# Turning the values and the heads' outputs by crossbar transfers and GpSimd copies in place of TensorE transposes

## The chip, the cores and the metric

The kernel runs on one core of a Trainium2 chip. Its engines work side by side: TensorE (PE, with its weight loads as PEld) multiplies, VectorE (DVE) and ScalarE (ACT) do elementwise work, GpSimd (POOL) does simple copies, and SyncE (SP) only issues DMAs. The time is that of one execution in device microseconds; the median of a few runs is given.

## What is computed

One layer of a hybrid backbone over 2048 latent tokens of width 1024, with a prefix of 256 context tokens. The part that the change touches is a bidirectional gated linear recurrence in eight heads of width 128. Cut to what matters:

```python
h = rmsnorm(x, norm_w) * (1 + scale) + shift          # (2048, 1024)
p = h @ w_in                                           # 9216 columns, f32
q, v, zf, zb = heads 0..7 of width 128, gate = the next 1024 columns
f = lb + (1 - lb) * sigmoid(z); k = 1 - f              # forward and backward
# chunkwise, per head and direction:
S_t = diag(f_t) S_{t-1} + k_t v_t^T;  o_t = S_t^T q_t
o = o_forward + o_backward                             # context first, from state 0
y_hg = o * rsqrt(mean(o*o) + eps) * onorm_w * silu(gate)
y_cv = gated short convolution of the other 4096 columns
x = x + gate_ada * (concat(y_hg, y_cv) @ w_out);  out = rmsnorm(x, final_norm_w)
```

## The kernel before

Every large product is written as three f16 products of a high and a low half, and pairs of 128-column blocks go through a seven-product scheme (`seven`, line 921), so that one unit is 7 products of 4 steps of 3 matmuls. The work is a list of windows (lines 1225 to 1311): 32 windows for eight heads times four segments of 512 tokens, then 4 windows for the first convolution block and 14 for the others, then the output projection. A window's units project the segment's gates, values and queries. Its `chain` is the scan of the segment before it, and its `extra` holds the second direction of the previous head, the scaling of its outputs and other side work. Heads alternate in the order of their segments, so that a window's operand tiles ("hops", nine buffers) are loaded as the last unit of the window before gives its buffers back (`prefetch`, line 1384).

The order is written out by a planner: every step has a weight (`PACE`, line 45), `merge_steps` (line 1437) spreads chain and extra over the window in proportion to their weights, and `tick` (line 1458) issues a step after the matmuls at its place. Each engine then works through its own instructions in that order. SyncE issues all DMAs concerned, also in that order, and an issue that has to wait for a buffer or a datum holds back those behind it.

The steps of one segment's scan (`scan_steps`, line 715) are these. `value_turn` (line 552): four TensorE transposes of 128x128 f32 (line 555) into PSUM and a ScalarE copy to SBUF (line 557), since the projection gives values with channels on partitions and the scan needs tokens there. `begin_levels`, then levels 0 to 6: each even level (`levels`, line 620) multiplies 32-wide blocks on TensorE (line 631), and every level updates the keys (`level_k`, line 485) and the queries (`level_q`, line 492) on VectorE in place. The odd levels 1, 3 and 5 (`held`, line 603) keep a copy of the keys by ScalarE (`km`, line 601) and one of the queries by GpSimd (`qm`, line 608) ahead of the update, for the matmuls of the next step. `level6` (line 641) collects the blocks with four small GpSimd copies (line 665). `key_turn`, `states` and `outp` turn the keys, form the states (line 681, which reads the values) and the outputs (line 737).

When a head's both directions are done, `y_steps` (line 813) scales a segment's output by its norm on ScalarE (line 825), turns it with four TensorE transposes (line 831), and VectorE multiplies the turned output in PSUM by the norm weight and the gate (line 833); `put_y` (line 751) takes its largest entry and stores it to DRAM.

Tiles come from rings: `ring` has ten buffers of 512 f32 per partition, and `pair` in the pool `hp` has four buffers, used by stores of the operand tiles (line 317) early on and by scans of the output weights (line 1016) in the windows of heads 6 and 7.

Of the kernel before, what the change touches and what calls it, by code (L numbers as in the profile page):

```python
# [10 lines left out]
F16 = mybir.dt.float16  # L11
BF16 = mybir.dt.bfloat16
I32 = mybir.dt.int32
U8 = mybir.dt.uint8
AF = mybir.ActivationFunctionType
ALU = mybir.AluOpType
# [3 lines left out]
P = 128  # L20
# [5 lines left out]
GW = 512  # L26
NG = SEQ // GW
NCH = GW // P
HK = KT // 2
HW = GW // 2  # L30
HOPS = 9
VQ_AT = 3
SMALL = {"cc": 16, "bada": 16, "nw": 8, "lg": 32, "onw": 1, "cw": 24}
HEADS = 8
HG = HEADS * P
# [15 lines left out]
def paced(weight, fn):  # L51

    return PACE.get(weight, weight), fn
# [7 lines left out]
def hybrid_layer(ctx: ExitStack, tc, x, cx, w_ada, b_ada, w_in, w_out, fnorm_w, small_d, masks, ident_d, sel_d, out):  # L61
    nc = tc.nc
    V, S, G, PE, SY = nc.vector, nc.scalar, nc.gpsimd, nc.tensor, nc.sync
# [8 lines left out]
    hp = hpg.__enter__()  # L72
# [24 lines left out]
    def px_t(nm):  # L97
        return px.tile([P, 512], F32, tag="px", name=nm)

    def ring(nm):  # L100
        return rp.tile([P, GW], F32, tag="ring", name=nm)
# [6 lines left out]

    def k_tile(nm):
        return scp.tile([P, 2, GW], F32, tag="K", name=nm)  # L110

    def flat(t):
        return t.rearrange("p a b -> p (a b)")
# [13 lines left out]
    def rsqrt(ss, n, inv_n, nm):  # L127
# [3 lines left out]
        V.tensor_scalar(v, ss, inv_n, EPS, ALU.mult, ALU.add)  # L131
        V.tensor_scalar(a.bitcast(I32), v.bitcast(I32), 1, None, ALU.logical_shift_right)
        V.tensor_scalar(y.bitcast(I32), a.bitcast(I32), -1.0, float(0x5F3759DF), ALU.mult, ALU.add)
        for _ in range(3):
# [5 lines left out]
    def pow2_scale(rs, nm, keep=False, room=0, rb=None):  # L140
# [7 lines left out]
        else:  # L148
            st = sp.tile([P, 4], F32, tag="scale", name=f"sc_{nm}", bufs=12)
        sti = st.bitcast(I32)  # L150
        V.tensor_scalar(sti[:, 2:3], ps[:, :1].bitcast(I32), 24, None, ALU.logical_shift_right)
        V.tensor_scalar(sti[:, 0:1], sti[:, 2:3], -EXP_UNIT, (204.0 - room) * EXP_UNIT, ALU.mult, ALU.add)
# [7 lines left out]

    small = cp.tile([P, sum(SMALL.values())], F32, name="small")
    SY.dma_start(small, small_d)
    par, at = {}, 0
    for nm_, n_ in SMALL.items():
        par[nm_] = small[:, at:at + n_]
# [4 lines left out]
    bada, nw, onw = par["bada"], par["nw"], par["onw"]  # L170
# [15 lines left out]
    def modulate(between, vq):  # L186
        pada = pa_t("pada")
        homes = [f_tile, k_tile, f_tile, k_tile, q_tile, q_tile] + [wa_hop] * 4

        def load(k):  # L190
            wa[k] = []
            for j in range(2):
                t = homes[(2 * k + j) % len(homes)](f"wa{k}{j}")
                t = t if len(t.shape) == 3 else t.rearrange("p (a b) -> p a b", a=2)
                SY.dma_start(flat(t), w_ada[0, k * P:(k + 1) * P, j * D:(j + 1) * D])
                wa[k].append(t)

        wa = {}
        room = len(homes) // 2
        for k in range(room):  # L200
            load(k)
            if k == VQ_AT:
                vq()
        for k in range(KT):
            for j in range(4):
                PE.matmul(pada[32 * j:32 * j + 32, :], sc32[:, k, :], wa[k][j // 2][:, j % 2],
                          start=k == 0, stop=k == KT - 1)
            if k + room < KT:
                load(k + room)
            between(k)  # L210
        return pada
# [261 lines left out]
    lb1 = cp.tile([P, 2, HEADS], F32, name="lb1")  # L473
    mask = qp.tile([P, NSUB, SB], U8, name="mask", bufs=1)

# [25 lines left out]
    def new_state(nm):  # L501
        return qp.tile([P, P], F32, tag="state", name=nm, bufs=10)
# [4 lines left out]
    class Seg:  # L507


        def __init__(s, hd, tok0, n, m, nm):  # L510
            s.hd, s.tok0, s.n, s.m, s.nm = hd, tok0, n, m, nm
            s.small = n < GW
            s.f = s.K = None

        def open_gates(s):
# [175 lines left out]
    def order(i, n):  # L691
        return list(range(n)) if i == 0 else list(range(n - 1, -1, -1))
# [22 lines left out]
    def scan_steps(h, s):  # L715
        prim = h.prim

        def states():
            pp = s.outer(prim)
            s.Ss = []  # L720
            Sp = h.S[prim]
            for ch in order(prim, NCH):
                s.Ss.append(Sp)
                Sn = new_state(f"S_{s.nm}_{ch}")
                V.scalar_tensor_tensor(Sn, Sp, s.decay(prim, ch), pp[:, ch * P:(ch + 1) * P], ALU.mult, ALU.add)
                Sp = Sn
            h.S[prim] = Sp
            psec = s.outer(1 - prim)
            s.Ts = scp.tile([P, GW], F32, tag="Tsec", name=f"Ts_{s.nm}", bufs=5)
            S.activation(s.Ts, psec, AF.Copy)  # L730

        def outp():
            po = px_t(f"o_{s.nm}")
            qo = (1 - prim) * GW
            for ch, Sp in zip(order(prim, NCH), s.Ss):
                sl = slice(ch * P, (ch + 1) * P)
                PE.matmul(po[:, sl], s.A[:, sl], s.v[:, sl], start=True, stop=False)
                PE.matmul(po[:, sl], s.qf[:, qo + ch * P: qo + (ch + 1) * P], Sp, start=False, stop=True)
            s.o = s.qf[:, qo:qo + GW]
            S.activation(s.o, po, AF.Copy)  # L740

        return ([paced("values", s.value_turn), paced("begin", s.begin_levels)]
                + [paced("levels", lambda: s.levels(0)), paced("held", lambda: s.held(1)),
                   paced("levels", lambda: s.levels(2)), paced("held", lambda: s.held(3)),
                   paced("levels", lambda: s.levels(4))]
                + [paced("held", lambda: s.held(5)), paced("level6", s.level6), paced("keys", s.key_turn), paced("states", states),
                   paced("out", outp)])

    ymax = cp.tile([P, 3 * HEADS, NG], F32, name="ymax")
# [1 line left out]
    def put_y(kt, g, y):  # L751
        V.tensor_reduce(ymax[:, kt, g:g + 1], y, mybir.AxisListType.X, ALU.max, apply_absolute_value=True)
        SY.dma_start(yT[g][:, kt, :], y)
# [59 lines left out]
    def y_steps(h, j, own_gate=False):  # L813
        s = h.segs[-1 - j]

        def gate():
            s.sg = qp.tile([P, GW], F32, tag="sg", name=f"sg_{s.nm}", bufs=2)
            SY.dma_start(s.sg, Gd[h.hd][:, s.tok0:s.tok0 + GW])

        def scale():  # L820
            if not own_gate:
                gate()
            for ch in range(NCH):
                sl = slice(ch * P, (ch + 1) * P)
                S.activation(s.o[:, sl], s.o[:, sl], AF.Copy, scale=h.rstd[:, j * NCH + ch:j * NCH + ch + 1])

        def turn():
            pt = px_t(f"oT_{s.nm}")
            for ch in range(NCH):
                sl = slice(ch * P, (ch + 1) * P)  # L830
                PE.transpose(pt[:, sl], s.o[:, sl], ident)
            y = ring(f"y_{s.nm}")
            V.scalar_tensor_tensor(y, pt, onw, s.sg, ALU.mult, ALU.mult)
            put_y(h.hd, s.tok0 // GW, y)

        return ([paced(0.0, gate)] if own_gate else []) + [paced("scale", scale), paced("turn_y", turn)]


    class Conv:
# [358 lines left out]
    for hd in range(HEADS):  # L1198
        h = Head()
        h.hd, h.prim, h.segs = hd, hd % 2, []  # L1200
        heads.append(h)
        h.ctx = Seg(hd, SEQ, CTX, 1, f"c{hd}")
        for i, g in enumerate(order(h.prim, NG)):
            s = Seg(hd, g * GW, GW, 0, f"{hd}_{g}")
            h.segs.append(s)

    def wkey(c0, c1, own=False):
# [19 lines left out]
    for wi, (kind, a, i) in enumerate(stretch):  # L1227
        units, chain, extra = [], [], []
        if kind == "head":
            h = heads[a]  # L1230
# [34 lines left out]
        if wi > 0 and stretch[wi - 1][0] == "head":  # L1265
            _, pa_h, pi = stretch[wi - 1]
            chain += scan_steps(heads[pa_h], heads[pa_h].segs[pi])
# [377 lines left out]
def _arrays(inputs):  # L1645
# [7 lines left out]
         "in_w_in": i_["w_in"][0].reshape(KT, P, -1, P).transpose(2, 1, 0, 3), "in_w_out": i_["w_out"],  # L1653
         "in_final_norm_w": i_["final_norm_w"], "in_small": np.concatenate([cols[n] for n in SMALL]).T}
    a.update(_constants())
# [3 lines left out]
def _constants():  # L1659
    p = np.arange(P)  # L1660
    diff = (p[:, None] % SB) ^ np.arange(SB)[None, :]
    m = np.zeros((P, NSUB, SB), np.float32)
    for lev in range(NSUB):
        m[:, lev, :] = (diff >> lev) == 1
    sel = np.zeros((P, 2, P), np.float32)
    for j in range(2):
        sel[[32 * j, 64 + 32 * j, 32 * j + 2], j, :] = 1.0
    return {"level_masks": m.reshape(P, NSUB * SB), "identity": np.eye(P, dtype=np.float32),
            "selector": sel.reshape(P, 2 * P)}
# [15 lines left out]
```

## Time and profile before

| | |
|---|---|
| Median of 3 runs | 2149.38 us (2148.78 to 2149.49) |
| The profiled execution (its span) | 2150.1 us |
| TensorE busy | 2073.2 us, 96% |
| VectorE busy | 1645.8 us, 77% |
| ScalarE busy | 1192.2 us, 55% |
| GpSimd busy | 191.8 us, 9% |
| Granted TensorE clock, mean | 0.994 |

Busy time is the union of an engine's instructions. A matmul's duration overlaps that of its neighbours in the pipeline, so the place that it takes in PE's order is read from the start of one to the start of the next. "Idle before, releaser" names what ended the idle time of an engine: for line 631 it may be GpSimd's copy of held queries or VectorE's update. The windows of the eight heads end near 1265 us; the turns that the change concerns begin with the eighth segment, near 374 us for the values.

### The profile page before, as it was taken

How to read it: one execution, taken by the hardware profiler on the slowest of the kernel's cores; microseconds unless marked ns; L12 is line 12 of the kernel's file. 1: busy time of each engine (PE TensorE's matmuls, PEld its weight loads, DVE VectorE, ACT ScalarE, POOL GpSimd, SP SyncE). 2: the span in 40 equal slices, each digit the busy share in tenths (PEclk: the TensorE clock that was granted, in tenths of full speed). 3: DMA queues.
4: the chain of work that ended last, by engine and by line, in shares of the span. 5: the costliest groups of instructions: out<-in, count | busy, mean ns of one | idle time of the engine just before them, and what ended most of it. 6: DMA issues, size and time to landing. Idle time of an engine off the chain costs nothing.

```text
span 2150.1 us, 53050 instructions
## 1 busy us (share of the span) xinstructions
PE 2073.2 (96%) x22111; PEld 1466.0 (68%) x22111; DVE 1645.8 (77%) x3413; ACT 1192.2 (55%) x2406; POOL 191.8 (9%) x272
## 2 busy tenths in 40 slices
PE   5988999999999999999999999999999999999998
PEld 2877878888888888888888887444444444444443
DVE  6787988878778787788687887678778656687775
ACT  7965666757567666576676654354445423333332
POOL 0121111111111110111110100000000000000000
PEclk9999999999999999999999999999999999999999
DMA  9567533442344233424543458933442105642421
GB/s 356 191 207 265 178 126 134 137 158 72 114 129 146 97 114 109 153 81 142 194 131 127 130 165 260 285 108 110 134 149 93 54 23 196 206 143 92 137 79 59
DMA packets 185798, 311.02 MB, mean 145 GB/s; under 512 B 13010, under 2 KB 114770, under 8 KB 183764
## 3 DMA queue, kind: packets, MB, share of 16 engines
q1 hardware_dynamic: 183396, 303.68, 42.9%
q8 instruction: 173, 2.83, 0.5%
q10 hardware_dynamic: 2160, 3.93, 0.5%
q14 instruction: 69, 0.57, 0.1%
HBM read 240.19 MB, written 67.37 MB: 143 GB/s over the span
## 4 chain that ended last, share of the span: by engine, by line
PE 65%; DVE 18%; ACT 7%; DMA 4%; issue 3%; POOL 1%; SPq 0%; POOLq 0%; ACTq 0%; DVEq 0%
PE sa L930 8%; PE sa L932 8%; PE sa L931 8%; PE sb L930 4%; PE sb L932 4%; PE sb L931 4%; PE sa_o L930 2%; PE sa_o L931 2%; PE sa_o L932 2%; DVE Q L492 2%; PE sc L930 2%; PE sc L931 2%; PE sc L932 2%; DVE K L485 2%; PE T L681 2%
## 5 line engine op out<-in xcount | busy, mean ns | idle before, releaser
L931 PEld LDWEIGHTS <-e_p 128*128 128x128 f16 x1332 | 130.4, 98 | 59.8 <-issue 10.3
L930 PEld LDWEIGHTS <-e_p 128*128 128x128 f16 x1332 | 130.4, 98 | 54.0 <-issue 1.1
L601 ACT ACTIVATE km<-K 128x512 f32<-128x512 f32 x192 | 129.6, 675 | 67.2 <-DVE K L485 61.1
L932 PEld LDWEIGHTS <-e_p 128*128 128x128 f16 x1332 | 130.3, 98 | 51.4
L485 DVE TENSOR_TENSOR K<-K,tot 128x512 f32<-128x512 f32 x192 | 132.2, 689 | 42.9 <-ACT km L601 25.3
L492 DVE TENSOR_TENSOR Q<-Q,tot 128x512 f32<-128x512 f32 x192 | 132.5, 690 | 34.9 <-POOL qm L608 19.5
L608 POOL COPY qm<-Q 128x512 f32<-128x512 f32 x96 | 80.8, 842 | 794.4 <-DVE Q L492 778.7
L931 PEld LDWEIGHTS <-whib_p 128*128 128x128 f16 x888 | 86.9, 98 | 42.1 <-issue 8.8
L930 PEld LDWEIGHTS <-whib_p 128*128 128x128 f16 x888 | 86.8, 98 | 36.7 <-issue 0.8
L930 PEld LDWEIGHTS <-whia_p 128*128 128x128 f16 x888 | 87.0, 98 | 35.7 <-DMA hop3B<-Hd3B 2.3
L932 PEld LDWEIGHTS <-wloa_p 128*128 128x128 f16 x888 | 87.0, 98 | 34.2
L931 PEld LDWEIGHTS <-whia_p 128*128 128x128 f16 x888 | 87.0, 98 | 33.9 <-issue 1.5
L932 PEld LDWEIGHTS <-wlob_p 128*128 128x128 f16 x888 | 86.8, 98 | 34.0
L157 ACT ACTIVATE e_p<-ws_p,sc_p 128x512 f16<-128x512 f32 x108 | 77.5, 718 | 54.9 <-DVE ws_p L444 42.0
L665 POOL COPY A<-Ac 32x128 f32<-32x128 f32 x128 | 77.2, 603 | 128.3 <-ACT A L661 110.6
L853 ACT ACTIVATE cv<-c,small 128x512 f32<-128x512 f32 (+1 forms) x36 | 24.2, 673 | 106.8 <-DVE c L871 61.1
L937 ACT ACTIVATE u<-sa,sx_w 128x256 f32<-128x256 f32 (+1 forms) x111 | 58.1, 524 | 43.5 <-PE sa L932 34.7
L937 ACT ACTIVATE p<-sa,sx_w 128x256 f32<-128x256 f32 (+1 forms) x111 | 57.4, 517 | 39.9 <-PE sa L932 39.8
L158 DVE SCALAR_TENSOR_TENSOR e_p<-ws_p,sc_p,e_p 128x512 f16<-128x512 f32 x108 | 79.4, 750 | 0.0
L409 ACT ACTIVATE junk<-ws_p 128x1024 f16<-128x1024 f32 x72 | 75.7, 1052 | 6.5 <-DMA ws_p<-in_w_in 6.3
L1596 POOL TENSOR_TENSOR x_o<-x_o,fw 128x512 f32<-128x512 f32 x1 | 1.3, 1262 | 868.0 <-ACT junk L1587 868.0
L937 ACT ACTIVATE p<-sb,sx_w 128x256 f32<-128x256 f32 (+1 forms) x111 | 57.8, 521 | 30.8 <-PE sb L932 28.0
(858 smaller groups left out, 7036.3 us busy)
## 6 DMA issues: line engine op xcount, KB each, us to landing
ws_p<-in_w_in SPq DMA_DIRECT2D x72, 512.0 KB, 4.3
y_o<-yT SPq DMA_DIRECT2D x32, 512.0 KB, 4.3
xt_x<-in_x SPq DMA_DIRECT2D x16, 512.0 KB, 6.2
wa<-in_w_ada SPq DMA_DIRECT2D x16, 512.0 KB, 10.2
Gd<-zs SPq DMA_DIRECT2D x32, 256.0 KB, 2.7
sg<-Gd SPq DMA_DIRECT2D x32, 256.0 KB, 4.4
wos<-in_w_out SPq DMA_DIRECT2D x32, 256.0 KB, 5.0
yT<-y SPq DMA_DIRECT2D x32, 256.0 KB, 2.9
```

What stands on the lines that cost most here:

```text
L157: S.activation(hi, src, AF.Copy, scale=st[:, 0:1])
L158: V.scalar_tensor_tensor(lo, src, st[:, 0:1], hi, ALU.mult, ALU.subtract)
L409: S.activation(junk.rearrange("p (k n) -> p k n", k=KT), stage[i], AF.Abs, accum_out=r)
L485: V.tensor_tensor(m, m, sub(cur, nb + 1, [[2, np_], [-(nb + 1), 2], [0, B]]), ALU.mult)
L492: V.tensor_tensor(m, m, sub(cur, 1, [[2, np_], [nb - 1, 2], [0, B]]), ALU.mult)
L601: S.activation(sub(s.km, 0, [[2 * B, n // (2 * B)], [B, 2], [1, B]]), mix(s.K, n, B, n // (2 * B)), AF.Copy)
L608: G.tensor_copy(sub(qm, 0, [[2 * B, n // (2 * B)], [B, 2], [1, B]]), mix(s.qf, n, B, n // (2 * B)))
L665: G.tensor_copy(A3[js, :, js], s.Ac[js])
L930: PE.matmul(ps, hi[:, k], rh, start=start and k == 0, stop=False, skip_group_check=not start)
L931: PE.matmul(ps, hi[:, k], right(name, 1, k), start=False, stop=False, skip_group_check=not start)
L932: PE.matmul(ps, lo[:, k], rh, start=False, stop=k == nk - 1, skip_group_check=not start)
L937: last_keep.append(S.activation(r, ps, AF.Copy, scale=sx))
```

## The change

Segments are numbered in the order of their windows, 0 to 31. From number 7 on, a segment is `fast`. Its values are then not turned by `value_turn` but by three steps. `over`: a transposing DMA through the crossbar, from the values seen as 1024 two-byte halves per partition to a tile of eight 128x128 blocks. `back`: four plain DMAs inside SBUF that bring the halves of one kind together, in runs of 256 bytes. `join`: a GpSimd copy that interleaves low and high halves to f32 again. The three stand around `begin_levels` and after level 1 in the chain. The same three steps turn the scaled output of fast segments of all heads but the last; the product with weight and gate then follows as a step of its own and reads SBUF. Context values, the first seven segments and the outputs of the last head are turned as before.

```diff
+U16 = mybir.dt.uint16
...
+BY_DMA = 7
...
+    def turn_steps(src, make, nm, after=(1.0, 1.0)):
+
+        t = {}
+
+        def over():
+            t["a"] = hp.tile([P, 2 * NCH, P], U16, tag="pair", name=f"ta_{nm}", bufs=4)
+            SY.dma_start_transpose(t["a"], src().bitcast(U16))
+
+        def back():
+            t["b"] = hp.tile([P, NCH, 2, P], U16, tag="pair", name=f"tb_{nm}", bufs=4)
+            for h in range(2):
+                for b in range(2):
+                    SY.dma_start(t["b"][64 * b:64 * b + 64, :, h, :], t["a"][h::2, b::2, :])
+
+        def join():
+            G.tensor_copy(make().bitcast(U16).rearrange("p (c d h) -> p c d h", c=NCH, h=2),
+                          t["b"].rearrange("p c h d -> p c d h"))
+
+        return [paced(after[0], over), paced(after[1], back), paced(0.3, join)]
...
+            s.fast = False
...
+        def new_value():
+            s.v = ring(f"v_{s.nm}")
+            return s.v
+
+        values = [paced("values", s.value_turn)]
+        held_v = []
+        if s.fast:
+            values, held_v = [], turn_steps(lambda: s.vT, new_value, f"v{s.nm}", (0.2, 0.2))
+        keys = [paced("keys", s.key_turn)]
+        return (values + held_v[:1] + [paced("begin", s.begin_levels)] + held_v[1:2]
+                + [paced("levels", lambda: s.levels(0)), paced("held", lambda: s.held(1))]
+                + held_v[2:] + [paced("levels", lambda: s.levels(2)), paced("held", lambda: s.held(3)),
                    paced("levels", lambda: s.levels(4))]
-                + [paced("held", lambda: s.held(5)), paced("level6", s.level6), paced("keys", s.key_turn), paced("states", states),
+                + [paced("held", lambda: s.held(5)), paced("level6", s.level6)] + keys + [paced("states", states),
                    paced("out", outp)])
...
-        return ([paced(0.0, gate)] if own_gate else []) + [paced("scale", scale), paced("turn_y", turn)]
+        def make():
+            s.oT = ring(f"oT_{s.nm}")
+            return s.oT
+
+        def product():
+            y = ring(f"y_{s.nm}")
+            V.scalar_tensor_tensor(y, s.oT, onw, s.sg, ALU.mult, ALU.mult)
+            put_y(h.hd, s.tok0 // GW, y)
+
+        end = [paced("turn_y", turn)]
+        if s.fast and h.hd < HEADS - 1:
+            end = turn_steps(lambda: s.o, make, f"o{s.nm}", (0.5, 0.5)) + [paced("turn_y", product)]
+        return ([paced(0.0, gate)] if own_gate else []) + [paced("scale", scale)] + end
...
             s = Seg(hd, g * GW, GW, 0, f"{hd}_{g}")
+            s.fast = hd * NG + i >= BY_DMA
```

More of the change, by code (lines that the diff above doesn't have):

```diff
@@ L740, in outp @@
             S.activation(s.o, po, AF.Copy)
-        return ([paced("values", s.value_turn), paced("begin", s.begin_levels)]
-                + [paced("levels", lambda: s.levels(0)), paced("held", lambda: s.held(1)),
-                   paced("levels", lambda: s.levels(2)), paced("held", lambda: s.held(3)),
+        def new_value():
[9 more added lines that the diff above has]
+                + held_v[2:] + [paced("levels", lambda: s.levels(2)), paced("held", lambda: s.held(3)),
                    paced("levels", lambda: s.levels(4))]
-                + [paced("held", lambda: s.held(5)), paced("level6", s.level6), paced("keys", s.key_turn), paced("states", states),
+                + [paced("held", lambda: s.held(5)), paced("level6", s.level6)] + keys + [paced("states", states),
                    paced("out", outp)])
```

## The prediction

> **What bounds the kernel now.** I read the page first, then busy time by stage, then who waits for whom, and last the few lines that the change touches in order of time.
>
> ```profile
> span 2150.1 us, 53050 instructions
> PE 2073.2 (96%) x22111; PEld 1466.0 (68%) x22111; DVE 1645.8 (77%) x3413; ACT 1192.2 (55%) x2406; POOL 191.8 (9%) x272
> PE 65%; DVE 18%; ACT 7%; DMA 4%; issue 3%; POOL 1%; SPq 0%; POOLq 0%; ACTq 0%; DVEq 0%
> ```
>
> The profiled execution's own time is its span, 2150.1 us, with nothing shown around it; that is 0.7 us over the median of the three timed runs, 2149.38. I take terms from the profile and set the sum against the median. TensorE carries the span, but a share of the whole says little about the stage that changes. The segments concerned are turned from about 374 us on and the scan ends near 1265 us, so I ask for that stretch:
>
> ```profile
> core 0: us, PE busy (x) PEld busy (x) DVE busy (x) ACT busy (x) POOL busy (x), PEclk, DMA share, GB/s
> 373.70:1265.00 891.30, 873.24 (x13437) 772.40 (x13436) 709.23 (x1565) 586.41 (x1334) 122.16 (x175) 1.00 0.39 127
> ```
>
> PE is busy 873.2 of 891.3 us (98%) at full clock, so 18 us is all it stands idle. VectorE is at 80%, ScalarE at 66%, GpSimd at 14%, the DMA engines at 39%. Work taken off PE here shortens the kernel, as long as nothing new makes PE wait. What PE waits for in the stretch, and who waits for GpSimd's copies of held queries (line 608, whole span):
>
> ```profile
> PE A L631 <- POOL qm L608: 6.1, 7, 2.7
> PE sa L930 <- ACT u L937: 3.0, 10, 0.6
> PE A L631 <- DVE Q L492: 1.9, 7, 0.3
> PE sa L930 <- DVE f L941: 1.8, 6, 0.5
> PE T L681 <- ACT kT L674: 1.6, 3, 0.8
> ...
> L608 POOL COPY qm<-Q x96: 604/655/2341, 107.5 to 1258.1; 128x512 f32<-128x512 f32 x96
> ...
>   DVE Q L492: 19.5, 42
>   PEld A L631: 14.1, 17
>   PE A L631: 9.7, 13
> ```
>
> Columns of the first five: total us, times, longest us. The engine that is idle most is the one that PE waits for longest. Of 96 held-query copies, 42 had VectorE waiting at their end and 17 + 13 = 30 had TensorE waiting: GpSimd is idle on the whole, but its few copies lie in the chain from VectorE to the next level's matmuls. That is where this change puts its new work.
>
> **What is removed.** By the loops there are 32 - 7 = 25 value turns (segments 7 to 31) and 21 output turns (segments 7 to 31 less the four of the last head) that change: 46 turns, each four 128x128 f32 transposes. A matmul's duration overlaps its neighbours', so I read the place that a turn takes in PE's order from start to start:
>
> ```profile
> 596.11 0.27 PE L932 MATMUL sb<-hop14T,wlob_p 128*128 128x256 f16 x1
> 596.22 0.60 PE L555 MATMUL vt<-ident,vT 128*128 128x128 f32 x4
> 596.65 0.27 PE L930 MATMUL sb<-hop14T,whib_p 128*128 128x256 f16 x1
> ...
> 608.04 0.60 PE L831 MATMUL oT<-ident,Q 128*128 128x128 f32 x4
> 608.48 0.27 PE L930 MATMUL sa<-hop14T,whib_p 128*128 128x256 f16 x1
> ```
>
> 596.65 - 596.22 = 0.43 us for values, 608.48 - 608.04 = 0.44 us for outputs. With 0.437, 46 turns are 46 x 0.437 = 20.1 us of PE, nearly all of it on the path since PE is 98% busy. This term is firm. ScalarE loses a copy per value turn, and VectorE's product of an output reads SBUF in place of PSUM:
>
> ```profile
> L557 ACT ACTIVATE v<-vt x32: 575/587/602, 104.8 to 1248.8; 128x512 f32<-128x512 f32 x32
> L833 DVE SCALAR_TENSOR_TENSOR y<-oT,small,sg x32: 705/751/753, 330.1 to 1330.9; 128x512 f32<-128x512 f32 x32
> L158 DVE SCALAR_TENSOR_TENSOR e_p<-ws_p,sc_p,e_p 128x512 f16<-128x512 f32 x48 | 34.9, 746 | 0.0
> ```
>
> ScalarE is freed of 25 x 0.587 = 14.7 us. I count it at nothing, because PE's two waits for ScalarE above are 3.0 + 1.6 us together; at best they go as well. The product stays at 0.75 us: line 158, with two SBUF inputs of the same size, takes 0.746. The copy it waited for moves, not its price.
>
> **What is added, GpSimd.** Each turn ends in a GpSimd copy of 1024 two-byte elements per partition that reads halves 256 bytes apart. No such copy is in the trace. The nearest rows:
>
> ```profile
> L665 POOL COPY A<-Ac x128: 284/653/1470, 124.8 to 1264.4; 32x128 f32<-32x128 f32 x128
> L569 DVE TENSOR_TENSOR ks<-K x32: 676/688/1097, 72.7 to 1235.9; 128x512 f32<-128x512 f32 x32
> ```
>
> Line 608 moves 512 elements in 0.604 us undisturbed, 1.18 ns each, so 1024 take 1.21 us; line 665 moves 128 in 0.284 us at best, 2.2 ns each, so 1024 take 2.27 us. I take 1.21, as line 608 is the long, strided copy and 665's price is mostly start-up, and keep 2.27 for the range. [...]
>
> What does a copy cost PE? Twice. First, GpSimd and VectorE hold each other up: line 608 takes 0.604 us alone and up to 2.341, line 569 0.688 and up to 1.097. So a new copy can hold back a VectorE instruction for its length. Second, GpSimd works in order: behind the values' copy stands the next held-query copy (level 3), for which the matmuls of level 4 wait. 30 of 96 such copies already had PE waiting. So for the 25 value copies I take 30/96 x 1.21 = 0.38 us each, 9.4 us; bounds are none at all, and 25 x 2.27 = 57 us with every copy on the path. Behind an output's copy no particular level stands; there it is VectorE that is held, and in the stretch PE waited for it 7 + 6 times in the rows above, against 1565 VectorE instructions. I take a tenth of the copy, 0.12 us, so 21 x 0.12 = 2.5 us, between none and 21 x 0.38 = 8 us.
>
> **What is added, transfers.** Each turn issues five DMAs on SyncE's queue: the crossbar transfer and four of 64 KB that put the halves in place. The four wait for the crossbar's landing, the crossbar for the values (or the scaled output), and everything later in SyncE's queue stands behind them. What stands there, and the time that the chain leaves:
>
> ```profile
> 624.10 0.32 SPq L1389 DMA_DIRECT2D hop17T<-Hd1T  x1
> 633.65 0.32 SPq L753 DMA_DIRECT2D yT<-y  x1
> 648.80 0.96 SPq L401 DMA_DIRECT2D ws_p<-in_w_in  x2
> ...
> 624.23 0.60 PE L555 MATMUL vt<-ident,vT 128*128 128x128 f32 x4
> 628.20 1.11 POOL L608 COPY qm<-Q 128x512 f32<-128x512 f32 x1 [14.45 <-DVE Q L492]
> 632.85 0.61 POOL L608 COPY qm<-Q 128x512 f32<-128x512 f32 x1 [3.54 <-DVE Q L492]
> ...
> 603.28 0.61 POOL L608 COPY qm<-Q 128x512 f32<-128x512 f32 x1 [2.14 <-DVE Q L492]
> 605.04 0.46 PE L631 MATMUL A<-qm,km 128*32 128x32 f32 x32
> ...
> out<-x_o SPq DMA_DIRECT2D x17, 256.0 KB, 2.1
> yT<-sg SPq DMA_DIRECT2D x64, 128.0 KB, 2.4
> xt_x<-in_x SPq DMA_DIRECT2D x16, 512.0 KB, 6.2
> ```
>
> After the last operand load of a window (624.10) SyncE issues nothing for 9.6 us, and then a store and weights for a later window: a wait of a few microseconds there delays nobody, so I price the queue at nothing; if that cover is missing (an output's transfers just ahead of an operand load), the load slips by that wait. From the value turn to the level-3 copy there are 632.85 - 624.23 = 8.6 us, in a short window 603.28 - 596.22 = 7.1. Two landings in a row with five issues take at least 5 x 0.32 + 2.1 + 2.1 = 5.8 us, at most, with 512 KB rows, 1.6 + 6.2 + 2.4 = 10.2. A 256 KB move inside SBUF is nearer to the low end, so I take 6 to 7 us: the copy then falls between the level-1 and level-3 copies and waits for nothing. Values, halves and turned outputs hold their buffers longer; I price that at nothing since the values' old place is freed by the landing, early in the window. A turn also takes two of the four pair buffers, which the scans of the output weights share in the windows of heads 6 and 7; the cover there is that a turn is over within some 9 us of a window of about 30, and without it a scan's load would hold SyncE until a copy is done.
>
> The sum: -20.1 + 9.4 + 2.5 = -8.2 us, 2149.4 - 8.2 = 2141.2.
>
> **The rivals.**
>
> *Nothing comes back.* The copies fall into idle stretches; the rows for it are GpSimd's 14% and VectorE's 80%. Then -20.1, and up to 4.6 more with the waits for ScalarE: 2125 to 2129. Against it: VectorE and GpSimd meet often, line 608's median being 0.655 and its longest 2.341.
>
> *The copy is long and eats the gain.* At 2.27 us: 25 x 30/96 x 2.27 = 17.7 and 21 x 0.23 = 4.8, together 22.5 against 20.1, 2151.8. Harder still: a level-3 copy that ends at 603.89 is used at 605.04, 1.15 us later; with every value copy in front, each costs 2.27 - 1.15 = 1.12, 28 us, and the end is 2149.4 - 20.1 + 28 + 4.8 = 2162. It decides from a copy of about 2 us.
>
> *The halves land late (slower).* If the two landings take longer than the 7.1 to 8.6 us, the copy waits on GpSimd with the level-3 copy behind it, and PE pays the difference 25 times. With the 10.2 us above and a copy of 1.21: 10.2 + 1.21 - 8.6 - 1.15 = 1.7 us, 42 us, so 2149.4 - 20.1 + 42 + 2.5 = 2174. For it: nothing in the trace shows a crossbar transfer. Against it: this is not HBM traffic and the DMA engines are 39% busy. [...]
>
> *PE's turns were not the bound.* If VectorE's chain sets the pace and the turns only filled its gaps, the 20 us become idle time and the end stays at 2149. PE's 98% speaks against it.
>
> **How the numbers follow.** About 0.2%, 4.3 us, is what a measurement of this kernel can tell from no change, so faster means under 2145.1, slower over 2153.7. The forecast (2133 to 2145) has 0.38, being the row-by-row sum; nothing comes back 0.17; the long copy 0.22, half of it within 0.2% and half above; late landing 0.18; not the bound 0.05. Faster: 0.38 + 0.17 = 0.55. Same: 0.11 + 0.05 = 0.16. Slower: 0.11 + 0.18 = 0.29. Cases of both signs hold most of the chance; the likeliest one's own range is 2133 to 2145. The range of 2127 to 2165 takes in the forecast, most of the first rival, the long copy and the mild part of late landing; outside lie about 0.05 below and 0.12 above.
>
> **What would show it.** Right: value turns on PE fall from 32 to 7 and output turns from 32 to 11, PE busy falls by about 20 us, and its idle time in the stretch grows from 18 us to about 30, the growth under waits for the level-3 copy and line 492. The new copy's mean duration decides between the forecast and the long copy; line 492's and 485's mean above 690 ns would show VectorE held. Late landing would show as GpSimd idle before the new copy, ended by a DMA, and as a time to landing of the crossbar transfer above 5 us. The forecast is wrong if PE's idle time does not grow at all, or grows by more than 20 us.

## The result, and the profile after

The changed kernel takes 2187.88 us (median of 4 runs, 2182.38 to 2192.66), the kernel before 2149.21 (2148.78 to 2149.49): a ratio of 1.0177, interval 1.0163 to 1.0192. The forecast was 2141.2, 8 us faster; the change is 38.7 us slower, and outside the range.

The profiled execution of the changed kernel took 2192.66 us, with a span of 2190.9. Its page, span, busy time and chain:

```profile
span 2190.9 us, 53120 instructions
PE 2069.5 (94%) x21927; PEld 1454.2 (66%) x21927; DVE 1672.4 (76%) x3413; ACT 1183.1 (54%) x2381; POOL 248.7 (11%) x318
PE 57%; DVE 22%; DMA 8%; ACT 8%; issue 3%; POOL 1%; SPq 1%; POOLq 0%; ACTq 0%; DVEq 0%
```

Two numbers stand out against the page before. TensorE executes 184 matmuls less (46 turns of four, as counted), yet its busy time falls by 3.7 us in place of 20. And VectorE, with the same 3413 instructions as before, is busy 26.6 us longer: the same work ran slower. TensorE's share of the chain falls from 65% to 57%, and VectorE and the DMAs take it over.

The stretch in which the turns changed, by the busy time of each engine (the columns are those of the same view in the prediction; the stretch is taken to 1300 us, since the scan ends later here). The first row is the kernel before, the second the changed one:

```profile
373.70:1300.00 926.30, 907.72 (x13744) 803.40 (x13743) 732.89 (x1631) 601.70 (x1389) 122.16 (x175) 1.00 0.41 132
373.70:1300.00 926.30, 867.59 (x13236) 758.38 (x13235) 734.05 (x1562) 576.93 (x1310) 176.41 (x216) 0.98 0.54 148
```

TensorE is idle 926.30 - 867.59 = 58.7 us, where it was 18.6 before. The granted clock is 0.98 where it was 1.00. The clock's record in this stretch has half clock for 34 us in eight pieces, where the kernel before has one piece of 3.4; half of the difference, 15 us, is close to the missing 16 us of busy time. What TensorE waited for (total us, times, longest), in the whole span, first in the kernel before, then in the changed one, whose lines 974 to 976 are the products of the units (930 to 932 before) and 981 the step that takes a finished product out of PSUM (937 before); the last row is VectorE's wait for the turned output:

```profile
PE A L631 <- POOL qm L608: 9.7, 13, 2.7
PE sa L930 <- ACT u L937: 3.6, 12, 0.6
...
PE A L650 <- POOL qm L608: 2.7, 2, 1.5
```

```profile
PE sa L974 <- ACT u L981: 25.9, 15, 5.8
...
PE A L654 <- POOL qm L631: 8.7, 9, 2.9
PE A L673 <- POOL qm L631: 6.4, 4, 3.1
PE sa L974 <- DVE f L985: 5.7, 7, 1.2
...
DVE y L874 <- POOL oT L129: 14.3, 5, 4.9
```

The wait for ScalarE's evacuation `u` (its copy of a product out of PSUM) grew from 3.6 us to 25.9, 21 of them in five long stops. The waits for GpSimd's held queries, on which the forecast had put the copies' price, grew only from 9.7 + 2.7 to 8.7 + 6.4 us. The longest stop is worth following back. The changed kernel in order of time, for SyncE, GpSimd, VectorE, ScalarE and TensorE in turn:

```profile
622.68 1.26 SPq L120 DMA_TRANSPOSE ta_v<-vT  x1
624.21 0.54 SPq L1434 DMA_DIRECT2D hop17T<-Hd1T  x1
627.60 3.50 SPq L126 DMA_DIRECT2D tb_v<-ta_v  x4
631.20 1.28 SPq L120 DMA_TRANSPOSE ta_o<-Q  x1
635.96 2.58 SPq L126 DMA_DIRECT2D tb_o<-ta_o  x4
...
632.86 1.15 POOL L129 COPY v<-tb_v 128x1024 uint16<-128x1024 uint16 x1 [3.90 <-DMA tb_v<-ta_v]
633.96 0.61 POOL L631 COPY qm<-Q 128x512 f32<-128x512 f32 x1
640.99 1.15 POOL L129 COPY oT<-tb_o 128x1024 uint16<-128x1024 uint16 x1 [6.43 <-DMA tb_o<-ta_o]
...
642.17 0.75 DVE L874 SCALAR_TENSOR_TENSOR y<-oT,small,sg 128x512 f32<-128x512 f32 x1 [4.89 <-POOL oT L129]
644.11 0.14 DVE L174 TENSOR_SCALAR sc_p<-sc_p 128x1 int32<-128x1 int32 x1
...
644.28 1.15 ACT L179 ACTIVATE whia_p<-ws_p,sc_p 128x1024 f16<-128x1024 f32 x1 [5.24 <-DVE sc_p L174]
645.34 0.46 ACT L981 ACTIVATE u<-sa,sx_w 128x256 f32<-128x256 f32 x1
...
645.84 0.37 PE L974 MATMUL sa<-hop15T,e_p 128*128 128x256 f16 x1 [5.80 <-ACT u L981]
```

Read it from below. TensorE stood 5.80 us for an evacuation; ScalarE had stood 5.24 us with that evacuation behind a weight split; the split's scale came from VectorE, which had stood 4.89 us at an output's product; the product waited for GpSimd's copy, the copy for its halves, and their first transfer was not issued until 631.20, though ScalarE had scaled the output by 602: the values' four transfers stood in SyncE's queue, waiting for their own crossbar landing. Stops on this same evacuation come at 797.63 (2.60 us), 945.66 (3.86), 1104.73 (3.11) and 1259.51 (5.59), once in each later head's window that turns two outputs.

The time a stop costs doesn't end with it. The granted clock (the column behind the five busy times) around the first:

```profile
641.00:644.40 3.40, 0.00 (x0) 0.00 (x0) 2.23 (x7) 0.12 (x1) 1.14 (x1) 0.99 0.34 68
644.40:651.20 6.80, 5.36 (x69) 3.51 (x72) 5.51 (x10) 3.23 (x5) 1.14 (x1) 0.50 0.22 64
651.20:654.60 3.40, 3.40 (x53) 2.99 (x43) 2.97 (x6) 1.68 (x3) 2.13 (x4) 1.00 0.00 0
```

After the empty 3.4 us the clock is half for 6.8; after the other four stops it is half for 3.4, 6.8, 3.4 and 3.4 us. The five pieces begin at 644.36, 797.96, 944.74, 1105.16 and 1258.76 us: three before their stop ends, two 0.3 and 0.4 us behind its end.

The new instructions themselves, by line (ns min/median/max), and their landings (us min/median/max), lines 129, 120 and 126:

```profile
L129 POOL COPY v<-tb_v x25: 1140/1149/2848, 369.4 to 1282.7; 128x1024 uint16<-128x1024 uint16 x25
L129 POOL COPY oT<-tb_o x21: 1146/1155/1607, 466.1 to 1296.1; 128x1024 uint16<-128x1024 uint16 x21
...
L120 SPq DMA_TRANSPOSE ta_v<-vT x25: 1247/1269/2449, 358.5 to 1274.0; - x25
...
DMA to landing us min/median/max: 3.1/3.9/7.4
...
L126 SPq DMA_DIRECT2D tb_v<-ta_v x100: 599/615/1788, 365.0 to 1280.4; - x100
...
DMA to landing us min/median/max: 2.2/2.6/6.6
```

The copy took 1.15 us (median; its mean is 1.28, since some were held), near the 1.21 of the forecast; the 2.27 of the long-copy rival doesn't hold for it. The crossbar transfer of 256 KB landed in 3.9 us, where the plain 256 KB store of the prediction's rows took 2.1. Issues cost more than priced: 1.27 and 0.615 us, in place of 0.32.

### The profile page after: what moved, and what is told of

Its sections match the earlier page's. It is cut to its first block, busy times and chain, and to the rows that moved or that the text cites. A ratio compares the mean times of both kernels' runs of the same rounds, so it can differ in the third digit from the quotient of the medians.

```text
span 2190.9 us, 53120 instructions
## 1 busy us (share of the span) xinstructions
PE 2069.5 (94%) x21927; PEld 1454.2 (66%) x21927; DVE 1672.4 (76%) x3413; ACT 1183.1 (54%) x2381; POOL 248.7 (11%) x318
## 4 chain that ended last, share of the span: by engine, by line
PE 57%; DVE 22%; DMA 8%; ACT 8%; issue 3%; POOL 1%; SPq 1%; POOLq 0%; ACTq 0%; DVEq 0%
PE sa L974 7%; PE sa L976 7%; PE sa L975 7%; PE sb L974 3%; PE sb L975 3%; PE sb L976 3%; DVE Q L514 2%; PE sa_o L974 2%; PE sa_o L975 2%; PE sa_o L976 2%; DVE K L507 2%; DMA ws_p<-in_w_in 2%; PE sc L974 2%; DVE e_p L180 2%; PE sc L975 2%
## 5 line engine op out<-in xcount | busy, mean ns | idle before, releaser
L975 PEld LDWEIGHTS <-e_p 128*128 128x128 f16 x1332 | 131.6, 99 | 84.3 <-issue 33.9
L514 DVE TENSOR_TENSOR Q<-Q,tot 128x512 f32<-128x512 f32 x192 | 142.2, 740 | 42.2 <-POOL qm L631 25.1
L974 PEld LDWEIGHTS <-whib_p 128*128 128x128 f16 x888 | 87.1, 98 | 38.7 <-DMA hop35T<-Hd3T 1.5
L179 ACT ACTIVATE hiS_o<-y_o,sc_y 128x1024 f16<-128x1024 f32 x32 | 36.8, 1151 | 71.6 <-PE sa_o L975 32.1
```

What stands on the lines that cost most here:

```text
L179: S.activation(hi, src, AF.Copy, scale=st[:, 0:1])
L514: V.tensor_tensor(m, m, sub(cur, 1, [[2, np_], [nb - 1, 2], [0, B]]), ALU.mult)
L974: PE.matmul(ps, hi[:, k], rh, start=start and k == 0, stop=False, skip_group_check=not start)
L975: PE.matmul(ps, hi[:, k], right(name, 1, k), start=False, stop=False, skip_group_check=not start)
```

## The experiments

Ratios are to the kernel before on the same chip, with 95% intervals; its median was 2148.0 to 2151.4. "The turns are out" means that neither TensorE nor a transfer turns the values and outputs concerned. Diffs are against the changed kernel unless another is named.

**First question: which half, and is it the transfers?** Theory after the profile: the late transfers hold the readers. Rival: the copies do it without them. The expectations call it "shared port"; no run shows a port, and the words stand for the author's theory that a copy holds VectorE.

e1, values only:

```diff
-        if s.fast and h.hd < HEADS - 1:
+        if False:
```

> Only the 25 value turns go by the crossbar; the outputs are turned by TensorE as before. Outputs' chain (the product on VectorE stands too few microseconds behind crossbar, four DMAs and GpSimd copy, and all of VectorE behind it): 25 x 0.437 = 10.9 us of PE saved, little given back, 2138 to 2148. Values' chain (the level-3 copy stands behind the late values' copy): the loss stays, above 2165. SyncE's queue (every issue and wait costs alike): some 25/46 of the loss stays, 2165 to 2172.

e2, outputs only:

```diff
-        if s.fast:
+        if False:
```

> Only the 21 output turns go by the crossbar; values are turned by TensorE as before. Outputs' chain: the whole loss and the values' saving missing, 2180 to 2198. Values' chain: 21 x 0.437 = 9.2 us faster than before, about 2140. SyncE's queue: some 21/46 of the loss, 2163 to 2170.

Measured: 2148.98 us, 1.0009 (0.9999 to 1.0018), and 2150.71 us, 1.0012 (1.0003 to 1.0021). Each half alone costs about what its turns give back; together they cost 1.77%. The loss is no sum over turns.

e3, the two output turns of a window interleaved, so that the second one's crossbar transfer is issued ahead of the first one's copy:

```diff
-                extra += y_steps(prev, 1) + y_steps(prev, 2)
+                y1, y2 = y_steps(prev, 1), y_steps(prev, 2)
...
+                    extra += y1[:2] + y2[:1] + y1[2:3] + y2[1:2] + y1[3:4] + y2[2:3] + y1[4:] + y2[3:]
```

> In windows with two output turns, their steps are interleaved, so that a product stands about 18 us behind its crossbar transfer in place of about 8; the work is the same. Outputs' chain: most of the loss goes, 2135 to 2155, with VectorE's wait for the turned output near nothing. Values' chain, SyncE's queue and the shared port: as the changed kernel, 2180 to 2195.

Measured: 2165.75 us, 1.0086 (1.0069 to 1.0103). More room for the landing is worth 0.91%, some 20 us, and 18.5 us of loss stay, between what either theory expected.

e4, no transfers; the GpSimd copy reads the unturned tile:

```diff
-            SY.dma_start_transpose(t["a"], src().bitcast(U16))
...
-                    SY.dma_start(t["b"][64 * b:64 * b + 64, :, h, :], t["a"][h::2, b::2, :])
+            t["b"] = src().bitcast(U16).rearrange("p (c d h) -> p c h d", c=NCH, h=2)
```

> Crossbar and plain transfers left out; GpSimd's copy reads the unturned tile, so values and outputs are not turned (other numbers come out). The GpSimd copies and the saved transposes stay. All theories in which the transfers are late or fill SyncE's queue: 20 us saved less what the copies cost, 2130 to 2142. Shared port (the copies hold VectorE): 2165 to 2190.

Measured: 2171.36 us, 1.0113 (1.0097 to 1.0128). Taking all 230 transfers away recovers 0.64%, some 14 us; the copies alone, with TensorE freed of the turns, still lose 1.13%. That the transfers are the whole cause falls here. These copies are not quite those of the changed kernel: they read every second half of a tile that is ready earlier, one in the same window (at 621.90) takes 1.33 us, where the changed kernel's fastest takes 1.14, and VectorE is busy 1684.1 us, longer than in the changed kernel.

**Second question: is it the place of the dependents?** e6 puts an output's copy and product into the next window; e8 also moves the values' four transfers behind level 0 and their copy behind level 4.

```diff
+        for join_, product_ in held_over:
+            extra += [paced(1.0, lambda: None), join_, paced(1.0, lambda: None), product_]
```

> The changed kernel, with an output's GpSimd copy and product issued in the window after its transfers, so that neither waits for a landing. Late product (VectorE stands behind a product that waits): VectorE's wait for the turned output goes to nothing and most of the 38 us with it, 2135 to 2150. Shared port: the copies are the same, so near the run without transfers, 2165 to 2175. SyncE's queue: 2175 to 2190.

> As the run with the product in the next window, and for the values the four plain transfers are issued after level 0 and the GpSimd copy after level 4, so that SyncE does not stand for the crossbar's landing and no held-query copy stands behind a late copy. If those waits of the values still cost, 3 to 10 us under the run with the product in the next window; if not, within 3 us of it.

Measured: 2179.84 us, 1.0132 (1.0115 to 1.0149), and 2175.21, 1.0123 (1.0099 to 1.0147). In e6 VectorE's wait for the product fell from 14.3 to 1.6 us and TensorE's for `u` from 25.9 to 9.9, yet TensorE stays idle 51.8 us in the stretch (926.30 less 874.47 busy): a later place removes most of these stops, but only some 10 us (0.45%) of the loss. e6 came out above the 2165 to 2175 us that was expected if the copies alone remained, and by the intervals e8 is not clear of it.

**Third question: each added part beside turns that are kept.** e5 adds the transfers to the kernel before, unread; e7 the copies, into a tile nobody reads; e12 puts a fill (a memset of the same size) in place of each copy; e9 adds the steps empty, with their weights.

```diff
-            values, held_v = [], turn_steps(lambda: s.vT, new_value, f"v{s.nm}", (0.2, 0.2))
+            held_v = turn_steps(lambda: s.vT, new_value, f"v{s.nm}", (0.2, 0.2))
...
-            end = turn_steps(lambda: s.o, make, f"o{s.nm}", (0.5, 0.5)) + [paced("turn_y", product)]
+            end = turn_steps(lambda: s.o, make, f"o{s.nm}", (0.5, 0.5)) + end
```

> The kernel before, with the 46 crossbar and 184 plain transfers added beside the TensorE turns; nothing reads what they bring, no GpSimd copy. SyncE's queue and DMA traffic (loads held up by issues, waits and packets): 2155 to 2175. Late product and shared port: nothing to wait for, 2147 to 2153.

> The kernel before, with the 46 GpSimd copies added beside the TensorE turns, at their places in the order, into a tile that nothing reads; no transfers. Shared port and GpSimd's order (a copy holds VectorE or the next held-query copy for its 1.15 us): 46 times some tenths, 2158 to 2175. Late product: no one waits for the copies, 2147 to 2154.

> The kernel before, with the added steps as empty entries of the planner's lists: the same work as before, only spread otherwise. If the added runs cost what they did (15 us for transfers, 19 us for copies) by shifting the other steps in the windows: 2160 to 2170. If by the transfers and copies themselves: 2147 to 2154.

> As the run with copies beside the turns, with a GpSimd memset of 1024 two-byte elements in place of each copy, which reads nothing. If the copies cost by holding VectorE's second input: back to the run with empty steps. If by standing ahead of held-query copies in GpSimd's order: as much as the copies in the share that the memset's length has of 1.15 us.

Measured: e9 2163.83 us, 1.0065 (1.005 to 1.008); e5 2166.36, 1.0074 (1.0059 to 1.0089); e7 2170.7, 1.0096 (1.0081 to 1.0111); e12 2173.5, 1.011 (1.0095 to 1.0125). The same instructions as before in a slightly different order (e9) cost 0.65%, so the others must be read against e9: transfers some 2 us, copies 7, fills 10. By this, copies look cheap and reads no worse than fills; but these kernels keep the turns, and the fifth question shows that the copies cost more without them. The fills say little: nothing holds them back, and 30 of the 46 ran between 319 and 351 us, ahead of the stretch.

**Fourth question: what is the removal worth?** e10 leaves the turns out and adds nothing, with the weights of the change; e11 the same with those of before.

```diff
-            G.tensor_copy(make().bitcast(U16).rearrange("p (c d h) -> p c d h", c=NCH, h=2),
-                          t["b"].rearrange("p c h d -> p c d h"))
+            make()
...
-            s.v = ring(f"v_{s.nm}")
-            return s.v
+            s.v = s.vT
```

> The turns left out and nothing put in their place (the scan reads unturned values, the product the unturned output, so other numbers come out); the planner's weights are those of the changed kernel. If PE's turns were on the path: 2128 to 2133. If they were not (VectorE's chain sets the pace): 2145 to 2152. If the spread of the steps costs as well: 2138 to 2147.

> As the run with nothing added, but with the planner's weights of the kernel before (an empty entry of 0.65 for the values, 0.54 for the product). Turns on the path: 2128 to 2133, and the difference to the run with the new weights is the cost of the spread, 0 if that costs nothing, 10 to 15 us if it does. Turns not on the path: 2145 to 2152.

Measured: 2136.88 us, 0.994 (0.9926 to 0.9955), and 2137.25, 0.9939 (0.9922 to 0.9956). The turns were on the path: 0.6%, some 13 us of the nominal 20.1, come back when they go, a smaller gain than the 2128 to 2133 us expected. With the turns out the weights make no difference (e11). From here on the base is e10: the change added 1.0177 - 0.994 = 2.37%, 51 us, to it; the copies and their readers (e4) 1.73%, 37 us.

**Fifth question: the copies or their readers?** All three kernels have the turns out and move nothing. Their copies start as soon as the values or the scaled output are there; e13's copies in order, the others read every second half, and none brings halves together from 256 bytes apart. e13 copies into a tile that nobody reads; e14 copies the values alone, read; e15 the outputs alone, read. Against e10, the copy of e13:

```diff
+            t["b"] = hp.tile([P, NCH, 2, P], U16, tag="pair", name=f"tb_{nm}", bufs=4)
+            G.tensor_copy(t["b"].rearrange("p c h d -> p (c h d)").rearrange("p (c d h) -> p c h d", c=NCH, h=2),
+                          src().bitcast(U16).rearrange("p (c d h) -> p c h d", c=NCH, h=2))
```

> The turns are left out and nothing is moved (values and outputs stay unturned); the 46 copies run on GpSimd into a tile that nobody reads. Theory (the copies' readers cost): the copies alone cost what they cost beside the kept turns, some 7 us, so about 2144 us, ratio 0.997. Rival (the copies themselves cost, by GpSimd's time and order, as soon as TensorE has less to do): about 2171 us, ratio 1.011, as with the read copies.

> The turns are left out and nothing is transferred (values and outputs stay unturned); only the 25 values are copied by GpSimd, and their readers wait for the copies; the outputs are left as they are. If the two kinds of copy cost alike (25 of 46 of 37 us): about 2157 us, ratio 1.003. If the outputs' product on VectorE is what costs: about 2142 us, ratio 0.996. If the two cost only together, back to back on GpSimd: this one and the other kind alone both stay under 2145.

> The turns are left out and nothing is transferred (values and outputs stay unturned); only the 21 outputs are copied by GpSimd, and the product on VectorE waits for the copies. If the two kinds cost alike: about 2154 us, ratio 1.002. If the product on VectorE is what costs: about 2165 us, ratio 1.007. If the two cost only together: under 2145.

Measured: e13 2168.7 us, 1.0084 (1.0068 to 1.01); e14 2159.39, 1.0043 (1.0029 to 1.0057); e15 2145.0, 0.9975 (0.9964 to 0.9986). My theory, that the copies' readers wait, falls: copies that nobody reads cost 1.44% over e10, 31 us, near the 37 of the read ones. The two kinds don't cost alike: 1.03%, 22 us, for the values and 0.35%, 8 us, for the outputs, where 2154 us were expected for e15. The page of e10 and that of e13, busy time:

```profile
PE 2053.8 (96%) x21927; PEld 1447.6 (68%) x21927; DVE 1645.3 (77%) x3413; ACT 1178.5 (55%) x2381; POOL 193.7 (9%) x272
```

```profile
PE 2059.5 (95%) x21927; PEld 1449.5 (67%) x21927; DVE 1679.2 (77%) x3413; ACT 1178.9 (54%) x2381; POOL 265.9 (12%) x318
```

Again VectorE's 3413 instructions took 33.9 us longer. Where, is seen in e13 in order of time, GpSimd first, then VectorE, then TensorE:

```profile
622.74 1.67 POOL L127 COPY tb_v<-vT 128x1024 uint16<-128x1024 uint16 x1 [9.14 <-DVE vT L981]
624.32 3.45 POOL L127 COPY tb_o<-Q 128x1024 uint16<-128x1024 uint16 x2
...
622.53 0.67 DVE L505 TENSOR_TENSOR K<-K,tot 128x512 f32<-128x512 f32 x1
623.12 1.77 DVE L455 TENSOR_TENSOR ws_p<-ws_p,ws_p 128x512 f32<-128x512 f32 x1
624.82 1.77 DVE L505 TENSOR_TENSOR K<-K,tot 128x512 f32<-128x512 f32 x1
626.52 2.28 DVE L588 TENSOR_TENSOR Q<-q,f 128x1024 f32<-128x1024 f32 x1
...
628.85 0.54 PE L652 MATMUL A<-Q,km 128*32 128x32 f32 x32 [3.18 <-DVE Q L588]
```

VectorE's line 505 (the keys' update) takes 0.67 us when it starts ahead of the copies and 1.77 when it starts beside them. Three instructions with two operands in SBUF (lines 455, 505 and 588) stand against three copies, each 1.05 to 1.1 us longer than the same three in e10 (0.67, 0.69 and 1.23), and TensorE stands 3.18 us behind the last. The wait for that product, over the span of e13:

```profile
PE A L652 <- DVE Q L588: 16.2, 6, 3.2
```

**Sixth question: the copy's reads, or its time in GpSimd's line?** e16 is e13 with each copy replaced by a copy of two halves and a fill of the other 1022. The small copy waits only for the first columns of its source, and the fill doesn't wait for the source at all:

```diff
-            G.tensor_copy(t["b"].rearrange("p c h d -> p (c h d)").rearrange("p (c d h) -> p c h d", c=NCH, h=2),
-                          src().bitcast(U16).rearrange("p (c d h) -> p c h d", c=NCH, h=2))
+            flat_b = t["b"].rearrange("p c h d -> p (c h d)")
+            G.tensor_copy(flat_b[:, 0:2], src().bitcast(U16)[:, 0:2])
+            G.memset(flat_b[:, 2:], 0)
```

> The turns are left out and nothing is moved (values and outputs stay unturned); in place of each unread copy of 1024 halves a copy of two halves, which waits for the same source, and a fill of the other 1022 (0.95 us by the memset row of the earlier run). Theory (the copy's reads hold VectorE's two-input instructions): VectorE's busy time stays near 1645 us, not 1679, and the time near 2140 us, ratio 0.996. Rival (the time in GpSimd's line is what costs): near 2165 us, ratio 1.007, with VectorE's busy time no matter.

Measured: 2131.13 us, 0.9916 (0.9902 to 0.993). The page of e16, busy time:

```profile
PE 2050.6 (96%) x21927; PEld 1445.8 (68%) x21927; DVE 1646.1 (77%) x3413; ACT 1178.7 (55%) x2381; POOL 245.7 (12%) x364
```

GpSimd is busy 52 us longer than in e10, the copies' readers don't exist, as in e13; VectorE is back at 1646.1, and all of the copies' cost is gone (1.68%, 36 us under e13). The time alone doesn't say that the reads did it, since the fills are shorter (0.95 us) and stand earlier, those of the window shown for e13 at 611.7 to 613.6 us in place of 622.7 to 626.0. VectorE's instructions beside a fill do say it; here the keys' update again, line 506, starts together with a fill:

```profile
1010.68 0.95 POOL L129 MEMSET tb_o<- 128x1022 uint16 x1
...
1010.68 0.69 DVE L506 TENSOR_TENSOR K<-K,tot 128x512 f32<-128x512 f32 x1
```

It takes 0.69 us, where it took 1.77 beside a copy. Over the traces, each VectorE instruction that overlaps an added one is set against the fastest of its kind in e10: beside e13's 46 copies 76 instructions are together 35.3 us longer, beside e16's 46 fills 111 are 2.1 us longer. In the changed kernel it is 28.8 us over 83 instructions. So it is the copies, which read, that lengthen VectorE's work, and the fills, which don't, hardly do: VectorE is busy 1679.2 us with the copies and 1646.1 with the fills. That this is all of the 31 us is likely, not shown, as the place changed too.

**Seventh question: does it help to take the copies off GpSimd?** e17 is the changed kernel with its copies on ScalarE; e18 is the same with the values alone, the outputs turned by TensorE as before.

```diff
-            G.tensor_copy(make().bitcast(U16).rearrange("p (c d h) -> p c d h", c=NCH, h=2),
-                          t["b"].rearrange("p c h d -> p c d h"))
+            S.activation(make().bitcast(U16).rearrange("p (c d h) -> p c d h", c=NCH, h=2),
+                         t["b"].rearrange("p c h d -> p c d h"), AF.Copy)
```

> The changed kernel with its 46 copies on ScalarE, which gave up the evacuations of the same turns, in place of GpSimd. If GpSimd's order (decay products and copies in one line) is what makes the readers late: most of the 37 us goes, and with some 14 us for the late transfers the time is about 2155 us, ratio 1.003. If any engine's copy behind a late transfer holds its own line the same way: 2180 us or more, since ScalarE's line also holds the evacuations that TensorE waits for.

> Only the values go through the transfers, and ScalarE, which no longer evacuates their turns, makes the copies; the outputs' turns stay on TensorE. Theory (the copies on GpSimd hold VectorE, and the values alone have slack for the late transfers): VectorE's busy time near 1648 us, and the time falls below the 2148.98 of the values alone with GpSimd's copies, to about 2142 us, ratio 0.997, as part of the 7 us that the unmoved half would leave. Rival (the transfers' lateness takes what the values' 25 turns give): 2149 us, ratio 1.000.

Measured: e17 2177.44 us, 1.0127 (1.0112 to 1.0142), 0.5% better than the change and far from the 2155 expected; e18 2141.38 us, 0.9965 (0.9952 to 0.9977), faster than both kernels. The waits of e17 within 373.7 to 1300 us:

```profile
PE sa L974 <- ACT u L981: 26.0, 14, 5.2
...
DVE y L874 <- ACT oT L129: 16.3, 5, 4.9
ACT oT L129 <- DMA tb_o<-ta_o: 14.6, 7, 3.5
```

With VectorE no longer held (1648.2 us busy; beside ScalarE's 46 copies 95 instructions are 2.3 us longer), five products stand 16.3 us, 14.3 in the changed kernel, and TensorE the same 26 us: these stops hang on when the outputs' halves land, for which the copies waited 14.6 us, not on who copies. In e18, with no output in the queue, the first of these rows falls to 6.9 us over the span. Its stretch:

```profile
373.70:1300.00 926.30, 908.62 (x13768) 804.12 (x13766) 746.59 (x1646) 620.34 (x1406) 120.17 (x175) 1.00 0.51 151
```

TensorE is idle 17.7 us and its clock is full, though ScalarE does 25 copies. e18 differs from e1 only in who copies the values: 0.44% less time, and VectorE busy 1651.2 us in place of 1663.1.

## Why the prediction was wrong

**The saving of 20.1 us.** Right in direction: 13 us by e10, 18 by e16. The rival that the turns were not the bound falls.

**The copy of 1.21 us.** Right: 1.15, 1.28 in the mean. So the long copy was not what ate the gain.

**The copies at 9.4 + 2.5 = 11.9 us. This step failed.** The mechanism stood in the text ("GpSimd and VectorE hold each other up ... a new copy can hold back a VectorE instruction for its length"), but it was sized by how often TensorE had waited for another copy, 30 of 96, and by "a tenth of the copy" for the outputs. The 30 also counts a copy twice where a matmul and its weight load both waited: the trace has 17 such copies, by which the term would have been 25 x 17/96 x 1.21 = 5.4 us, further off. Measured, with copies of nearly the same kind: 31 us unread, 37 read; values 22, outputs 8. The wrong thought was in the path: the wait for held queries, which was priced, grew by 2.7 us, while VectorE's whole line, from which TensorE's next weights and level products come, grew by 33.9 us over 46 copies in e13, 0.74 us each, and by 26.6 in the changed kernel. How much of it reaches TensorE differs: 22 of 23.2 us in e14, 8 of 20.1 in e15, and with the turns kept 7 of 25.8 in e7 over e9. The row that would have said so was quoted: line 608's longest at 2.341 and line 569's at 1.097.

**The transfers at nothing.** Also failed: e4 puts them at 14 us on top of the copies. The cover named, 9.6 us without issues on SyncE, held for the operand loads; what was missed is that the output's transfers stand behind the values' in that queue, and that "behind an output's copy no particular level stands" left out its own product, with VectorE's whole line behind it. The rival of late halves expected a landing over 5 us and the values' levels as payers; it was 3.9 us, the five issues took 3.9 (1.28 + 2.58) to 4.8 (1.26 + 3.50), and the outputs paid.

**How the two add up.** Over e10, copies without transfers cost 37 us, transfers without copies on GpSimd (e17) 40, both 51. Either alone loses more than the turns give, which is why taking one away repaired little: from the changed kernel, leaving out the transfers gives 14 us and moving the copies off GpSimd 11. Part of e17's 40 may be ScalarE's own 46 copies; it was not separated, so how the 51 us divide between the two stays open.

**The clock.** The sum had no term for it. TensorE's busy time should have fallen by 20.1 us and fell by 3.7; the half clock accounts for some 15 of the 16 between, out of the 41 us by which the span grew. Five of its eight pieces begin within the five long stops or up to 0.4 us behind them.

**The signs named.** Idle time was to grow to about 30 us, and a growth of more than 20 was to show the forecast wrong; it grew by 40, to 58.7. Means above 690 ns in lines 492 and 485 were to show VectorE held; the same lines in the new kernel, 514 and 507, have 740 and 703.

What stays open: beside kept turns a fill cost as much as a copy (e12 and e7), though only the copies lengthened VectorE's work (1671.4 and 1645.7 us busy). Most of those fills stood ahead of the stretch, and e9 shows that order alone can move this kernel by 0.65%, which is also the size of the 14 us given to the transfers; what costs in e12 wasn't tried.

## What to carry to other kernels

Before work goes to an idle GpSimd, look at what VectorE does beside it, since part of GpSimd's time can become VectorE's: here 46 copies, 58.7 us in sum, made VectorE's total 26.6 us longer. In the changed kernel line 801, with its operands in SBUF, took 1.27 us beside a copy (at 1012.72) where its fastest took 0.31; line 748, of the same size with one operand in PSUM, took 0.34 beside each of four copies, its median; line 153, which reads a single tile in SBUF, took 0.87 beside each of the same four, where its fastest took 0.17. VectorE's busy total with an unchanged instruction count is the number that shows it. A transfer chain is priced with what stands ahead of it in its own queue (here an output's transfer issued at 631.20, though the output was ready by 602) and with the first instruction that reads it, on whichever engine, since what stands behind that instruction waits too (VectorE 4.89 us, then ScalarE 5.24 and TensorE 5.80). Test a part with the bottleneck relieved (turns out, part in), since beside the old load it may look cheap (the copies: 7 us beside kept turns, 31 without).

## What the runs showed of the hardware that was not expected

- VectorE's 128x512 update of the keys took 1.77 us when it started beside a GpSimd copy and 0.67 when it started ahead of one; the copies there took 1.67 and, two in a row, 3.45, where one of e4's of the same size took 1.33. Beside a fill of 1022 halves (0.95 us) the update took 0.69.
- A crossbar transfer of 128x1024 two-byte elements took 1.27 us to issue and 3.9 to land (3.1 to 7.4); a 64 KB move inside SBUF with strided blocks 0.615 us to issue, twice the 0.32 of the loads.
- ScalarE made the interleaving copy of 1024 halves in 1.17 us, where GpSimd took 1.15, and beside its 46 copies 95 VectorE instructions were only 2.3 us longer in sum.
- With each of five stops of TensorE of 2.6 to 5.8 us went 3.4 or 6.8 us at half clock, begun before its end or up to 0.4 us behind it, and not the longer the stop (3.86 us: 6.8; 5.59 us: 3.4).
